# Streams of small matmuls resumed by a running account of all engines, in place of fixed sleeping times

## The chip, the cores and the metric

The kernel runs on one core of a Trainium2 chip. The time is the device time of one execution in microseconds, and the kernel before is told by the median of three runs. A core has five engines that this text names: PE (TensorE, the matmuls; PEld is its loading of weights), DVE (VectorE), ACT (ScalarE), POOL (GpSimd) and SP (SyncE, which issues most DMAs). Each works through its own instructions in order, and waits by semaphore for what others produce.

## The reference

One step of a two-layer encoder trunk. A prompt of 1024 frames with 16 meta tokens ahead of it, and 8 running streams of 16 frames, 1168 columns in all, pass through each layer. A layer normalises its input, projects it to many heads, and runs three kinds of mixers side by side: latent attention (8 heads), mLSTM (4 heads) and gated DeltaNet (4 heads); their outputs are gated and projected back. The two recurrences go chunk by chunk, each chunk needing the state of the one before:

```
def step(S, xs_c):                                       # gated DeltaNet
    A   = where(strict, b * (k @ k^T) * gamma, 0)
    u,w = triangular_solve(A + I, [b * v, b * exp(G) * k])
    delta = u - w @ S
    o = (q * exp(G)) @ S + ((q @ k^T) * gamma) @ delta
    S = exp(G_last) * S + (k * exp(G_last - G))^T @ delta
    return S, o

def step((C, n, m), xs_c):                               # mLSTM
    m_t = max(b + m, max_s dmat);  w_inter = exp(b + m - m_t)
    qk  = (q @ k^T) * exp(dmat - m_t)
    num = w_inter * (C @ q) + qk @ v;  den = w_inter * (n @ q) + sum(qk)
    h   = num / max(|den|, exp(-m_t))
    C, n = g_state * C + v g_tok k^T,  g_state * n + g_tok k
```

Everything is float32 in and out. The outputs are the activations of both kinds of streams, the new latents and rotary keys, and the states.

## The kernel before, in words

The frames are kept transposed: 128 features on the partitions, 1168 columns in three slices (400, 384, 384). The recurrences use one meta chunk of 16 columns, eight chunks of 128 (0 to 8) and one for the samples (9).

*Dense work.* Most of PE's time is the projection of the layer's input (`projs`, `part`, L610 and following): for each 128 output features and each slice 24 accumulating matmuls into a PSUM tile `pa`, with weights split into a high part (`wh`, fp32r) and bfloat16 (`wb`). The output projection (`out_first`, `out_proj`) is of the same kind. This chain, `main()`, is called the filler.

*Streams.* Everything else is a generator: `gates` (L709, gates and decays of all heads), `gdn(h)` (L895, one DeltaNet head), `mlstm(h)` (L1191), `gfin` and `mfin` (finish of a batch of chunks), `rstd`, `normx`, `normy` (the norms, L476 to L565), and attention (`prep`, `gload`, `att_m`, `att`, `samp_*`). A stream records instructions and then says `yield y`: it wants to sleep for y microseconds.

*What sets the order.* `Weave.run` (L269 to L305) writes everything out before the chip runs. It keeps a planned time of PE, `W.t`, which only `mm` and `tr` (L360 to L374) advance, each by a guess from the size. It takes the first stream in its list whose sleep is over; if there is none, three dense matmuls. So a sleep is the amount of other PE work that is put between a step and the next one. The order of recording is the priority by which a list scheduler then orders each engine, and `gate` (L378) ties some DVE, ACT, POOL and SP instructions to the place on PE after which they were recorded.

*A chunk step of `gdn`* (L1097 to L1168): k·S and q·S into `psS`; DVE forms r0 from it (L1124); two transposes of the next chunk (`pre`); sleep YA = 0.84; PE multiplies the inverse U with r0 (L1129); DVE scales the result to dl (L1131); sleep YB = 0.70; PE multiplies kd and dl (L1135), DVE forms the new state (L1140); sleep 0.7. A step of `mlstm` has one such exchange through DVE (L1278, from PSUM; sleep YM = 0.8).

*The inverse* of a DeltaNet head: DVE solves blocks of 16 rows (L950 to L966); the two results T and U go to DRAM (`td`, `ud`) and come back in another layout (L970 to L974; sleeps 9.0, 2.12 and 5.00), ACT and DVE mask them (L982, L983), and six merge steps (L990 to L1050) join blocks of 16 to 32, 64 and 128, each a group of small matmuls, one DVE or ACT operation on its result, and a sleep YI = 2.5. Other fixed sleeps are YF = 7.70 ahead of `finish` (L882, its matrix work waits for L1176 to L1320's scales), YT = 5.30, YN = 9.20 and 2.70 in the norms (ahead of the broadcast of the scales, whose operand L508 makes), 0.45 to 8.0 in `gates` (L820 is DVE's in it).

`split` (L436) makes the high and low part of a loaded weight; its second half runs on DVE or POOL (L441).

## Time and profile before

| | |
|---|---|
| median of three runs | 2652.36 us (2650.05 to 2653.49) |
| the profiled execution, whole | 2655.11 us |
| its span, first to last instruction | 2653.3 us |
| PE busy | 2494.3 us, 94% of the span |
| DVE, ACT, POOL busy | 58%, 42%, 29% |
| granted TensorE clock, mean | 0.976 |

A busy share over the whole span hides stages, so the rows further below also show two windows of 50 us, one of them in attention. The line numbers in the profile are those of the kernel before; `L361` is the matmul helper, `L372` the transpose helper, so matmuls of all streams carry these lines, and are told apart by their tiles and by who releases them. `pa` are PSUM tiles of dense work, `pb` those of streams, `wk` working tiles, `pg` pages, `sm` small columns.

### The profile page before, as it was taken

To read this page: it belongs to the slowest core of one execution; us is meant where nothing else is said; L and a number is where in the kernel's file an instruction comes from. 1 tells how busy PE (TensorE), PEld (TensorE's weight loads), DVE (VectorE), ACT (ScalarE), POOL (GpSimd) and SP (SyncE) were. 2 spreads that over 40 slices of the span, in tenths; PEclk is the share of its full clock that TensorE was granted. 3 is DMA by queue.
4 is the path that set the end of the run, shared out by engine and by line. 5 is a ranking of instruction groups with operands and counts; after the bars stand their busy time and mean duration, and the time that the engine had idled before them with its cause. 6 is when DMAs were issued, how large, how long until landed. Compare 5 with 4: busy or idle time off the path is not lost. (4 is left out here: it accounts for less than half of the span.)

```text
span 2653.3 us, 45522 instructions
## 1 busy us (share of the span) xinstructions
PE 2494.3 (94%) x17310; PEld 2154.2 (81%) x17310; DVE 1529.8 (58%) x3716; ACT 1115.5 (42%) x2635; POOL 763.2 (29%) x865
## 2 busy tenths in 40 slices
PE   6999999999999999979998999999999999999997
PEld 4887888878878888779977888788788788887896
DVE  6667465465453476655565784755743526665636
ACT  5363444444442433443343544444444434334612
POOL 3112222122123542232341222221221245322414
PEclk9999999999999999989999999999999999998998
DMA  3212112121113734464422121221211255444832
GB/s 130 67 40 76 51 52 83 51 69 49 60 59 113 201 105 122 124 215 160 153 79 57 43 74 52 61 73 51 69 52 57 84 148 162 116 115 149 281 117 80
DMA packets 158411, 258.67 MB, mean 97 GB/s; under 512 B 48704, under 2 KB 110768, under 8 KB 158192
## 3 DMA queue, kind: packets, MB, share of 16 engines
q1 hardware_dynamic: 152224, 247.59, 30.2%
q0 software_dynamic: 1856, 3.86, 0.7%
q10 hardware_dynamic: 4112, 4.30, 0.7%
q8 instruction: 137, 2.24, 0.4%
q14 instruction: 82, 0.67, 0.1%
HBM read 190.77 MB, written 64.92 MB: 96 GB/s over the span
## 5 line engine op out<-in xcount | busy, mean ns | idle before, releaser
L361 PE MATMUL pa<-pg,wh 128*128 128x384 f32 (+3 forms) x6324 | 1320.5, 352 | 25.5 <-DVE wk L1423 8.8
L361 PEld LDWEIGHTS pa<-pg,wh 128*128 128x128 f32 x6324 | 1108.2, 190 | 69.4 <-DVE wk L1423 9.4
L361 PE MATMUL pb<-pg,pg 128*128 128x352 f32 (+26 forms) x1908 | 427.4, 339 | 17.7 <-DVE sm L1552 4.4
L361 PE MATMUL pa<-pg,wb 128*128 128x384 bf16 (+1 forms) x2208 | 422.1, 331 | 6.2 <-POOL pg L544 4.2
L361 PEld LDWEIGHTS pb<-pg,pg 128*128 128x128 f32 (+7 forms) x1908 | 302.5, 189 | 71.1 <-issue 14.9
L361 PEld LDWEIGHTS <-wb 128*128 128x128 bf16 x2208 | 202.0, 98 | 142.4 <-issue 30.4
L361 PE MATMUL pb<-wk,pg 128*128 128x128 f32 (+4 forms) x2168 | 224.2, 250 | 21.2 <-ACT wk L983 5.5
L441 POOL TENSOR_TENSOR wh<-wf,wh 128x1024 fp32r<-128x1024 f32 (+1 forms) x61 | 144.1, 2363 | 325.1 <-ACT wh L437 318.7
L361 PEld LDWEIGHTS pb<-wk,pg 128*128 128x128 f32 (+3 forms) x2168 | 195.2, 162 | 43.0 <-issue 16.8
L1589 ACT ACTIVATE wk<-pb 128x320 f32<-128x320 f32 (+8 forms) x288 | 113.9, 406 | 244.9 <-PE pb L361 221.4
L361 PE MATMUL pa<-wk,pg 128*128 128x320 f32 (+8 forms) x576 | 192.5, 420 | 1.8 <-ACT wk L1589 1.3
L437 ACT CAST wh<-wf 128x1024 fp32r<-128x1024 f32 (+1 forms) x122 | 126.4, 1036 | 126.0 <-PE pa L361 110.7
L1552 DVE TENSOR_REDUCE sm<-pb 128x1 f32<-128x348 f32 (+9 forms) x232 | 107.8, 493 | 102.3 <-PE pb L361 89.6
L1612 DVE RECIPROCAL wk<-pa 64x320 f32<-64x320 f32 (+2 forms) x48 | 110.6, 2305 | 51.1 <-PE pa L361 50.4
L361 PE MATMUL pb<-wk,wk 32*32 32x16 f32 (+6 forms) x1776 | 110.7, 216 | 15.3 <-POOL wk L1285 5.6
L868 DVE SCALAR_TENSOR_TENSOR pg<-pg,vec,pg 128x1192 f32<-128x1192 f32 x72 | 107.2, 1504 | 18.3 <-ACT pg L866 18.0
L1530 POOL TENSOR_TENSOR pg<-pg,pg 64x520 fp32r<-64x520 f32 (+1 forms) x64 | 87.0, 1370 | 104.8 <-ACT pg L1529 91.1
L693 ACT COPY pg<-pa 128x384 f32<-128x384 f32 (+1 forms) x108 | 52.0, 481 | 134.4 <-PE pa L361 133.2
L457 ACT CAST wb<-wf 128x1024 bf16<-128x1024 f32 x92 | 96.2, 1045 | 26.3 <-PE pa L361 20.6
L441 DVE TENSOR_TENSOR wh<-wf,wh 128x1024 fp32r<-128x1024 f32 (+1 forms) x61 | 78.9, 1293 | 47.3 <-ACT wh L437 47.0
L361 PEld LDWEIGHTS pa<-wk,pg 128*128 128x128 f32 (+1 forms) x576 | 98.8, 195 | 5.9 <-ACT wk L1589 1.8
L361 PEld LDWEIGHTS pb<-wk,wk 32*32 32x32 f32 (+2 forms) x1776 | 73.2, 122 | 33.9 <-issue 9.4
(298 smaller groups left out, 3196.3 us busy)
## 6 DMA issues: line engine op xcount, KB each, us to landing
wf<-win SPq DMA_DIRECT2D x92, 512.0 KB
pg<-latT SPq DMA_DIRECT2D x32, 520.0 KB
pg<-latN SPq DMA_DIRECT2D x32, 512.0 KB
wf<-wout SPq DMA_DIRECT2D x24, 512.0 KB
xa<-wk SPq DMA_DIRECT2D x40, 192.0 KB
mix<-pg SPq DMA_DIRECT2D x12, 584.0 KB
pg<-mix SPq DMA_DIRECT2D x12, 584.0 KB
mix<-pg SPq DMA_DIRECT2D x12, 576.0 KB
```

Of the source, the lines that this page charges most:

```text
L361: W.last = P.matmul(out, lhsT, rhs, start=start, stop=stop)
L437: S.copy(hi, src)
L441: lo_eng.tensor_sub(lo, src, hi.bitcast(F32))
L457: S.copy(wb[:, :n], wf)
L693: S.copy(o[:, s0:s1], ps)
L868: V.scalar_tensor_tensor(y[:, :n], cb[:, j:j + n], vcol(l, "cw", 4 * ti + j), y[:, :n], op0=ALU.mult, op1=ALU.add)
L1530: G.tensor_sub(lo, raw, hi.bitcast(F32))
L1552: V.tensor_reduce(mx[:LEN[c], 3 * c + i_:3 * c + i_ + 1], ps[:LEN[c], :n1 - x_], axis=AX.X, op=ALU.min)
L1589: S.activation(pt[:m, :b - a], ps, AF.Exp, scale=-1.0)
L1612: V.reciprocal(rc, po[d, :w])
```

## The change

The planned time is replaced by an account of every engine. `Clocks` keeps the time at which each written range of a tile is expected to be done, a clock for PE, and lists of busy stretches for DVE, ACT, POOL and SP, into whose gaps a new instruction is fitted. `Engine` wraps each engine's interface, so every recorded instruction is entered with a cost by its size. `due(tiles)` gives the time at which these tiles are expected, and `due()` the time at which the last instruction that this step recorded is; a stream that yields it sleeps until `W.t` reaches that. `ring` makes a new PSUM or working tile wait for the one whose place it takes. `W.t` is now PE's clock in the account, so it also grows by PE's expected waits, and matmul costs are set anew.

Fixed sleeps that become `due`: those of the norms, `gates`, `gdn`, `mlstm`, `gfin` and `mfin`. Those of attention and of the sample streams stay in numbers. No instruction is added or removed; all of them keep their operands, save that four halves of `split` change engine, as it alternates between two.

```
+class Clocks:
+    HOP = 90.0
...
+    def run(self, eng, outs, ins, ns, late=0.0, queue=None):
+        t = max([0.0] + [self.ready(a) + self.HOP for a in ins]
+                + [self.after.get(self.where(a)[0], 0.0) for a in outs])
+        if eng == "PE":
+            t = max(t, self.clk["PE"])
+            self.clk["PE"] = t + ns
+        else:
+            t = self.fit(eng, t, ns)
+        e = t + ns
+        if queue is not None:
+            e = max(e, self.clk.get("dma", 0.0)) + queue
+            self.clk["dma"] = e
+        e += late
+        for a in outs:
+            self.write(a, e)
...
+        if eng != "PE":
+            self.last = max(self.last, e)
+        return t
...
+class Engine:
+    COST = {"DVE": (150.0, 1.08), "ACT": (224.0, 0.83), "POOL": (200.0, 2.1)}
...
+            if name == "dma_start":
+                n = aps[0].size() if callable(aps[0].size) else aps[0].size
+                c.run(kind, outs, ins, 60.0 if kind != "POOL" else 600.0, 1900.0, n * 4 / 260.0)
+            else:
+                n = max(x.free_size() for x in aps)
+                b, m = self.COST[kind]
+                ns = b + m * n
...
+                c.run(kind, outs, ins, ns, 60.0)
...
 class Weave:
...
                     r = next(th[0])
-                    if isinstance(r, (int, float)):
+                    if isinstance(r, At):
+                        th[1] = max(r, self.t)
+                    elif isinstance(r, (int, float)):
                         th[1] = self.t + r * 1000.0
...
+    def due(*aps):
+        return At(max([CK.ready(a) for a in aps]) + CK.HOP) if aps else At(max(CK.last, W.t) + CK.HOP)
...
         elif rhs.dtype != F32:
-            W.t += max(n / 2.4, 107.0)
+            ns = max(n * 0.4375 + 7.0, 107.0)
...
+    def pe(out, a, b, ns):
+        CK.clk["PE"] = W.t
+        CK.run("PE", [out], [a, b], ns, 160.0)
+        W.t = CK.clk["PE"]
...
-        yield 2.70
+        yield due(dg)
...
-            yield 9.0
+            yield due()
             ld(td.rearrange("c (b i) j -> (c b) (i j)", b=8), Ti)
             ld(ud.rearrange("c (b i) j -> (c b) (i j)", b=8), Ui)
-            yield 2.12
+            yield due()
             Tc, Uc = AD, ip[:, 928:1088].rearrange("p (c j) -> p c j", j=16)
             ld(Tc, td.rearrange("c s j -> s c j"))
             ld(Uc, ud.rearrange("c s j -> s c j"))
-            yield 5.00
+            yield due()
...
-            yield YI
+            yield due()
...
-                    yield YA
+                    yield due(r0)
...
-                    yield YB
+                    yield due(dl)
...
-                    yield 0.7
+                    yield due(Sst) if c < 9 else 0.7
...
-            yield YF
+            yield due(Ob)
...
-                    yield YM
+                    yield due(*([V1, VG] + ([CN] if c else [])))
```

What this does to the order is shown at three places. In these rows `L361`, `L372` and `L383` of the kernel before are `L491`, `L503` and `L340` of the changed one, and tile numbers differ between the two.

PE, layer 0, a chunk step of DeltaNet head 2. `pb809` of the kernel before is k·S and q·S (two matmuls), `pb810` the transposes, `pb819` U·r0; `pa` are dense matmuls. Before:

```order
L361 MATMUL pb809_5181<-wk807_5168,pg591_3737 128x128
L361 MATMUL pb809_5181<-wk807_5168,pg714_4360 128x128
L372 MATMUL pb810_5185<-cst_92,pg669_4083 128x128
L372 MATMUL pb810_5185<-cst_92,pg591_3737 128x128
L361 MATMUL pa798_5127<-pg15_122,wh751_4844 128x384
L361 MATMUL pa798_5127<-pg16_123,wh751_4844 128x384 x2
L361 MATMUL pa818_5219<-pg9_116,wh777_4999 128x400 x2
L361 MATMUL pa818_5219<-pg10_117,wh777_4999 128x400
L361 MATMUL pb819_5223<-wk802_5146,pg732_4563 128x128
```

In the changed kernel the same step is `pb808`, `pb809` and `pb812`:

```order
L491 MATMUL pb808_5120<-wk806_5107,pg600_3781 128x128
L491 MATMUL pb808_5120<-wk806_5107,pg714_4359 128x128
L503 MATMUL pb809_5124<-cst_92,pg684_4126 128x128
L503 MATMUL pb809_5124<-cst_92,pg600_3781 128x128
L491 MATMUL pa803_5098<-pg9_116,wh764_4900 128x400
L491 MATMUL pa803_5098<-pg10_117,wh764_4900 128x400 x2
L491 MATMUL pb812_5134<-wk793_5064,pg739_4608 128x128
```

Between the transposes and U·r0 stood six dense matmuls; now there are three.

PE, layer 1, the first merge of DeltaNet head 1. The 32 matmuls of `32x32` are the first product, the two groups of `32x16` use its masked result. Before:

```order
L361 MATMUL pb_16279<-wk_16237,pg_15886 32x32 x32
L361 MATMUL pa_16266<-pg_13452,wh_16122 128x384 x2
L361 MATMUL pa_16266<-pg_13453,wh_16122 128x384 x2
L361 MATMUL pa_16266<-pg_13454,wh_16122 128x384 x2
L361 MATMUL pa_16266<-pg_13455,wh_16122 128x384 x2
L361 MATMUL pa_16266<-pg_13456,wh_16122 128x384 x2
L361 MATMUL pa_16266<-pg_13457,wh_16122 128x384 x2
L361 MATMUL pa_16327<-pg_13450,wh_16122 128x384 x2
L361 MATMUL pa_16327<-pg_13451,wh_16122 128x384 x2
L361 MATMUL pa_16327<-pg_13452,wh_16122 128x384 x2
L361 MATMUL pb_16334<-wk_16312,wk_16237 32x16 x32
L361 MATMUL pb_16368<-wk_16237,wk_16312 32x16 x32
```

The same in the changed kernel, where the `32x32 x16` behind them begins the next merge:

```order
L491 MATMUL pa_16605<-pg_13450,wh_16392 128x384 x2
L491 MATMUL pb_16193<-wk_16171,pg_15805 32x32 x32
L491 MATMUL pa_16605<-pg_13451,wh_16392 128x384 x2
L491 MATMUL pa_16605<-pg_13452,wh_16392 128x384 x2
L491 MATMUL pb_16240<-wk_16226,wk_16171 32x16 x32
L491 MATMUL pb_16274<-wk_16171,wk_16226 32x16 x32
L491 MATMUL pb_16322<-wk_16171,pg_15805 32x32 x16
L491 MATMUL pa_16605<-pg_13453,wh_16392 128x384 x2
L491 MATMUL pa_16605<-pg_13454,wh_16392 128x384 x2
L491 MATMUL pb_16350<-wk_16226,wk_16171 32x32
L491 MATMUL pb_16350<-wk_16171,wk_16226 32x32
```

Between first product and second stood 18 dense matmuls, and now four; the next merge follows the second product with none between.

SP, layer 1, DeltaNet head 0: the way of T and U through DRAM. `td1_0` and `ud1_0` are the DRAM buffers, `MR1` another row of the gates, `wf` a weight's landing tile. Before:

```order
L383 DMA pg2578_14664<-MR1 128x9x128
L383 DMA td1_0<-pg2560_14431 80x256
L383 DMA ud1_0<-pg2560_14431 80x256
L383 DMA pg2578_14664<-MR1 128x16
L453 DMA wf2594_14881<-win 128x1024
L383 DMA pg2560_14431<-td1_0 128x10x16
L383 DMA pg2560_14431<-ud1_0 128x10x16
```

In the changed kernel:

```order
L340 DMA pg2578_14660<-MR1 128x9x128
L340 DMA pg2578_14660<-MR1 128x16
L340 DMA wf2596_14908<-win 128x1024
L340 DMA td1_0<-pg2556_14385 80x256
L340 DMA ud1_0<-pg2556_14385 80x256
L340 DMA pg2556_14385<-td1_0 128x10x16
L340 DMA pg2556_14385<-ud1_0 128x10x16
```

The stores of T and U stand behind the second load of `MR1` and the weight load, and their loads follow at once.

## Rows read from the trace of the kernel before

**Rows 1.** Head of the profile page: span, busy time and share by engine.

```profile
span 2653.3 us, 45522 instructions
...
PE 2494.3 (94%) x17310; PEld 2154.2 (81%) x17310; DVE 1529.8 (58%) x3716; ACT 1115.5 (42%) x2635; POOL 763.2 (29%) x865
```

**Rows 2.** Waits of PE by releaser: total us, times, longest us.

```profile
PE pb L361 <- DVE wk L508: 19.5, 17, 4.6
...
PE pb L361 <- POOL wk L1285: 5.6, 4, 2.3
PE pb L361 <- ACT wk L983: 5.5, 1, 5.5
...
PE pb L361 <- DVE wk L1131: 4.5, 6, 2.2
...
PE pb L361 <- POOL wk L1956: 3.8, 2, 2.8
...
PE pb L372 <- DVE pg L820: 3.4, 1, 3.4
PE pb L361 <- DVE wk L1278: 3.3, 3, 1.7
...
PE pb L361 <- DVE sm L923: 2.7, 1, 2.7
PE pb L372 <- DVE wk L1320: 2.5, 3, 1.2
...
PE pb L361 <- DVE wk L1140: 2.0, 4, 0.9
PE pb L361 <- DVE wk L1124: 2.0, 3, 1.4
```

**Rows 3.** PE's timeline, first and last stage: start, us, instruction, [idle before].

```profile
16.75 1.22 PE L361 MATMUL pb<-wk,onesr 128*128 128x400 f32 x2 [4.62 <-DVE wk L508]
...
2641.51 1.01 PE L361 MATMUL pb<-cst,wk 128*128 128x1 f32 x4 [2.82 <-POOL wk L1956]
2644.90 0.82 PE L361 MATMUL pb<-wk,onesr 128*128 128x256 f32 x2 [2.38 <-DVE wk L508]
```

**Rows 4.** Timeline of all engines, second loads of the inverse, layer 1.

```profile
1444.15 0.43 SPq L383 DMA_DIRECT2D pg<-td  x1
...
1449.93 1.08 PE L361 MATMUL pb<-wk,pg 32*32 32x32 f32 x64 [5.51 <-ACT wk L983]
```

**Rows 5.** Timeline of all engines, one chunk step of the gated DeltaNet, head 2.

```profile
466.71 0.61 PE L361 MATMUL pb<-wk,pg 128*128 128x128 f32 x4
...
467.29 1.31 PE L361 MATMUL pa<-pg,wh 128*128 128x384 f32 x6
467.36 0.35 DVE L1124 SCALAR_TENSOR_TENSOR wk<-pb,sm,wk 128x128 f32<-128x128 f32 x1 [0.84 <-PE pb L361]
...
468.44 0.38 PE L361 MATMUL pb<-wk,pg 128*128 128x128 f32 x2
```

**Rows 6.** Timeline of all engines, one merge of the inverse, layer 0.

```profile
586.17 0.42 DVE L997 TENSOR_TENSOR wk<-pb,cst 128x256 f32<-128x256 f32 x1
...
588.97 1.21 PE L361 MATMUL pb<-wk,wk 32*32 32x16 f32 x120
```

**Rows 7.** Timeline of all engines, end of a batch of chunks.

```profile
223.02 2.36 POOL L441 TENSOR_TENSOR wh<-wf,wh 128x1024 fp32r<-128x1024 f32 x1
223.09 2.31 DVE L1176 TENSOR_TENSOR sm<-sm 128x4 f32<-128x4 f32 x1 [0.88 <-POOL sm L1175]
```

**Rows 8.** Groups by line and shape: count, busy us, mean ns, idle before.

```profile
L1176 DVE TENSOR_TENSOR sm<-sm 128x1 f32<-128x1 f32 x12 | 1.9, 161 | 7.5 <-POOL sm L1175 7.5
...
L441 POOL TENSOR_TENSOR wh<-wf,wh 128x1024 fp32r<-128x1024 f32 x57 | 136.8, 2400 | 318.5 <-ACT wh L437 312.1 <-DVE wk L1890 6.3
```

**Rows 9.** Busy time by window (us, share): a recurrence and an attention stretch.

```profile
300.00:350.00 50.00, 49.66 (x351) 42.44 (x351) 24.80 (x79) 23.63 (x67) 7.69 (x10) 1.00 0.14 45
1150.00:1200.00 50.00, 43.09 (x294) 41.41 (x294) 24.20 (x44) 22.24 (x56) 16.74 (x27) 0.85 0.60 198
```

More of the change, by code (lines that the diff above doesn't have):

```diff
@@ L248, in unpack, with __init__, where, ready @@
     )
+class At(float):
+    pass
+class Clocks:
+    HOP = 90.0
+    def __init__(self):
+        self.clk = {}
+        self.busy = {}
+        self.done = {}
+        self.seen = {}
+        self.after = {}
+        self.last = 0.0
+    @staticmethod
+    def where(a):
+        t = a.tensor
+        if a.space.name == "DRAM":
+            return t.name, a.offset, a.offset + 1 + sum((n - 1) * abs(s) for s, n in a.ap)
+        lo = a.offset % a.ap[0][0]
+        hi = lo + 1 + sum((n - 1) * abs(s) for s, n in a.ap[1:])
+        return t.name, lo, hi
+    def ready(self, a):
+        name, lo, hi = self.where(a)
+        return max([e for x, y, e in self.done.get(name, ()) if x < hi and lo < y], default=0.0)
+    def write(self, a, e):
+        name, lo, hi = self.where(a)
+        self.done[name] = [w for w in self.done.get(name, ()) if not (lo <= w[0] and w[1] <= hi)] + [(lo, hi, e)]
+    def run(self, eng, outs, ins, ns, late=0.0, queue=None):
[13 more added lines that the diff above has]
+            self.write(a, e)
+        for a in ins + outs:
+            n = self.where(a)[0]
+            self.seen[n] = max(self.seen.get(n, 0.0), e)
+        if eng != "PE":
+            self.last = max(self.last, e)
+        return t
+    def fit(self, eng, t, ns):
+        q = self.busy.setdefault(eng, [])
+        while len(q) > 200:
+            q.pop(0)
+        k = len(q)
+        while k and q[k - 1][0] >= t:
+            k -= 1
+        if k and q[k - 1][1] > t:
+            t = q[k - 1][1]
+        while k < len(q) and q[k][0] < t + ns:
+            t = max(t, q[k][1])
+            k += 1
+        q.insert(k, (t, t + ns))
+        return t
+    def follows(self, new, old):
+        if old is not None:
+            self.after[new] = self.seen.get(old, 0.0) + self.HOP
@@ L308, in _build @@
 def _build(nc, tc, ctx, I, O, layers):
-    V, S, G, P = nc.vector, nc.scalar, nc.gpsimd, nc.tensor
+    W = Weave()
+    CK = W.clocks
+    V, S, G = (Engine(e_, n_, CK) for e_, n_ in ((nc.vector, "DVE"), (nc.scalar, "ACT"), (nc.gpsimd, "POOL")))
+    P, SY = nc.tensor, Engine(nc.sync, "SP", CK)
+    def due(*aps):
+        return At(max([CK.ready(a) for a in aps]) + CK.HOP) if aps else At(max(CK.last, W.t) + CK.HOP)
     cp = ctx.enter_context(tc.tile_pool(name="const", bufs=1))
@@ L823, in gates @@
             D1["MR"] = 1
-            yield 1.23
+            yield due()
             ps = pb()
@@ L909, in gdn @@
             V.memset(hs, 1.0)
-            yield 8.0
+            yield due(kT)
             yield from need(1)
@@ L1061, in gdn @@
             QD = D
-            yield 4.0
+            yield due(qT)
             for b in BATCHES:
```

119 lines of the change are left out of this document (73 added, 46 removed).

## Prediction

> **What bounds the kernel now.** I read the head of the page first, then PE's waits by releaser, then timelines around the waits and around one step of each kind, then the groups by shape and two windows. PE is busy 2494.3 of 2653.3 us [rows 1]: at most 159.0 us can be won, and only where PE waits. A step that a stream finishes sooner gives nothing by itself, because the same matmuls are still to be done; a step that is put too close behind its operand costs the whole difference, because PE takes its instructions in order. So the change is priced by two lists: waits of PE that an earlier or later place takes away, and steps whose cover of dense matmuls becomes too thin.
>
> The waits that belong to streams with a new sleep are the eleven rows of [rows 2]: 19.5 + 5.6 + 5.5 + 4.5 + 3.8 + 3.4 + 3.3 + 2.7 + 2.5 + 2.0 + 2.0 = 54.8 us. Three of their instances lie where no dense work is left to put between, at the beginning and at the end: 4.62 + 2.82 + 2.38 = 9.8 us [rows 3]. That leaves 45.0 us in reach. The other waits, such as those for attention, keep their fixed sleeps. A recurrence stretch has PE at 49.66 of 50 us and an attention stretch at 43.09 [rows 9], so where most of the new sleeps are there is least to win.
>
> **Waits that go.** Every time below is that of the profiled execution, 2655.11 us; it lies 2.75 above the median of 2652.36, and I take that off at the end.
>
> Three waits stand alone, and the changed order removes the cause of each. The longest is 5.51 us, where the masking on ACT waits for T to come back from DRAM, a load issued at 1444.15 and used at 1449.93 [rows 4]. Two fixed sleeps, 2.12 and 5.00, stand for that way; the account prices each DMA and puts 31 to 50 us of PE work between the solve and the first merge, where 28 to 31 stood (both counted from the order at the durations of the trace). That the stores now stand behind one weight load on SP delays them by one issue of that queue, about 0.4 us as the issue in [rows 4], and the added cover is larger. The second is 3.4 (L820, a step of `gates`), the third 2.7 (L923, ahead of `finish`) [rows 2]. Together 5.5 + 3.4 + 2.7 = 11.6 us, taken in full.
>
> The rest, 45.0 − 11.6 = 33.4 us, is 12.5 us of L508 (19.5 less 4.62 and 2.38), the L1285, L1320 and L1956 rows, and the chunk steps. The account knows the operand of each (`due(dg)`, `due(r0)`, `due(vB)`), so its expectation should fit where a fixed number was too short; but it knows nothing of what the list scheduler moves afterwards, and it charges by size alone. I take half, 16.7 us. Bounds: none and all, that is 0 and 33.4.
>
> Sum of what goes: 28.3 us, between 11.6 and 45.0 if the three are sure, from 0 if they are not.
>
> **Waits that come.** First the chunk steps. Around U·r0 the row of before reads: products ready at about 467.32 (466.71 + 0.61), DVE's L1124 from 467.36 for 0.35, so r0 at 467.71; PE takes it at 468.44 [rows 5]. Slack 0.73 us, with six dense matmuls of 1.31 us between [rows 5]. The order of the changed kernel has three there, so half of that 1.31, 0.65 us, is gone: slack 0.08. So a typical step still just fits, and nothing is lost by it; but any other DVE operation ahead of L1124 now shows. Over both layers, four heads and the chunks these steps are 72 of L1131, 72 of L1124 and 64 each of L1140 and L1278, 272 in all, of which the rows of before count 6 + 3 + 4 + 3 = 16 waits with 4.5 + 2.0 + 2.0 + 3.3 = 11.8 us, 0.74 each [rows 2]. The median cover in the order falls from six to three at L1124 and L1140, stays six at L1131 and falls from nine to four in `mlstm`. I take as many again as there were: 16 × 0.74 = 11.8 us. Bounds: 0, if the expectation is good to 0.08 us on average; and, if DVE is found at work by every second of the 200 steps with thinner cover (its busy share is 58% [rows 1]) and each then costs 0.74, 100 × 0.74 = 74 us.
>
> Second the merges. Before, DVE's mask takes 0.42 us from 586.17 and the next product starts at 588.97 [rows 6]: 588.97 − 586.59 = 2.38 us of slack. In the order, covers of 17 or 18 dense matmuls become 2 to 10. At the 0.22 us of one dense matmul (1.31 over six [rows 5]) ten are 2.2 and two 0.4 us, against a need of about half a microsecond. Of 8 heads × 6 = 48 steps I take every sixth to wait half a microsecond: +4. Bounds 0 and 48 × 0.5 = 24.
>
> `finish` has a cover of 5 to 8 us after against nearly 10 before; its operand chain on DVE and POOL needs less than that in most rows, and I add nothing beyond the rest above. Sum of what comes: 11.8 + 4 = 15.8, bounds 0 and 98.
>
> **Kept as it is, but shifted.** Attention and samples keep their numbers, yet sleep against a `W.t` that also counts PE's waits, so a given number now covers less PE work. An attention window has 50 − 43.09 = 6.9 us without PE [rows 9]; one and a half such windows more or less make ±10. I take 0, since neither sign is shown. The granted clock there is 0.85 and in a recurrence stretch 1.00 [rows 9]; the order of work in attention is hardly touched, so I price no change of it. Four halves of `split` change engine; 2.40 us each on POOL [rows 8], and neither engine is the bound: nothing.
>
> **Sum.** 2655.1 − 28.3 + 15.8 = 2642.6; less 2.75 this is 2640 us by the runs' median.
>
> **What the account cannot see.** POOL's half of a weight split began at 223.02 for 2.36 us, and a DVE operation on four columns that began at 223.09 took 2.31 [rows 7], where the same line on one column takes 0.161 on average over 12 [rows 8]. It ended with the other: a stall of 2.15 us that depends on when the two meet. The account charges DVE by columns and never meets POOL. The Trainium skill ("SBUF — State Buffer", section "Who interferes with whom") says that a DVE instruction with two SBUF inputs and a GpSimd one that reads SBUF exclude each other, and that the one issued second blocks fully. That row agrees. By the rule the thinner covers are wrong whenever a split runs; by the sum above they are wrong only at random.
>
> **Rivals.**
>
> *Slower, by stalls of DVE behind POOL's splits under thin covers.* There are 57 such splits of 2.40 us [rows 8]. Before, a slack of 0.7 to 2.4 us [rows 5, 6] hid part of a stall; after, 0.08 hides none. POOL is busy 29% of the span [rows 1]; if one split in three catches DVE ahead of a step, that is 19 × 2.15 = 41 us more: 2655.1 − 28.3 + 15.8 + 41 − 2.75 = 2681. It decides from 12.5 / 2.15, about six such catches, on. For it: the row of 223.09, and the halved covers. Against it: the L1124 and L1140 steps read one operand from PSUM, so they are stopped only when an operation ahead of them on DVE is.
>
> *No change, given back.* Only the three single waits go (11.6) and the chunk steps bring 11.8: −11.6 + 11.8 = 0, 2652. For it: half of what I let go in the rest rests on the account being right, and the list scheduler still moves about a fifth of the matmuls away from where they were recorded, after as before.
>
> *All of the reach.* The account is right everywhere and no new wait comes: 2652.4 − 45.0 = 2607. For it: the sleeps before were one number for all instances of a step. Against: 16 of 272 chunk steps waiting is already a low share.
>
> **How the numbers follow.** Forecast 2640 (its own range 2630 to 2650, by the ±10 of attention): 0.38. All of the reach, 2607: 0.12. No change: 0.20. Slower: 0.30. A difference under 0.2% (5.3 us) is what a measurement of this kernel cannot tell from no change. Faster by more: 0.38 + 0.12 = 0.50; within: 0.20; slower: 0.30. The range reaches from the full reach to the slower rival, 2607 to 2681, and leaves out the upper bounds of the new waits (98 us) and a gain in stages that I did not price, together about 0.2.
>
> **What would show it.** The first product of the inverse in layer 1, head 0, no longer waits for L983's counterpart, and the L820 and L923 waits are gone (the 11.6). L508's row falls from 19.5 towards 7 us plus half of 12.5, some 13. The chunk rows (L1131, L1124, L1140, L1278) stay near 16 to 25 waits and below 20 us; over 50 us in them and longer DVE operations beside POOL's splits would make the slower rival true. The merge steps show waits of half a microsecond where none were. PE's busy time stays within some us of 2494. I am wrong if the attention windows change by more than 10 us, or if the gain comes from where PE did not wait for a stream with a new sleep.

## The result and the profile after

The changed kernel is slower: 2695.1 us in the median of four runs (2691.2 to 2701.8), against 2651.2 for the kernel before in the same comparison; the ratio is 1.0168, with a 95% interval of 1.0143 to 1.0194. The forecast was 2640 and its range ended at 2681.

The head of the page, as in [rows 1]:

```profile
span 2690.3 us, 45584 instructions
...
PE 2517.2 (94%) x17310; PEld 2168.1 (81%) x17310; DVE 1534.6 (57%) x3716; ACT 1115.8 (41%) x2635; POOL 774.4 (29%) x865
```

PE's time without work is span less busy: 2690.3 − 2517.2 = 173.1 us, 14.1 more than the 159.0 of before. But busy time grew as well, by 2517.2 − 2494.3 = 22.9 us, for the same 17310 matmuls. The mean granted clock fell from 0.976 to 0.967. The share of the span that the lower clock takes is 0.024 × 2653.3 = 64 us before and 0.033 × 2690.3 = 89 after, which is 25 more. So of the 37.0 us by which the span grew, about 14 are waits and about 23 are work at a lower clock. The other executions agree on the clock: in all four of the changed kernel its mean is 0.963 to 0.967, in the fifty of the kernel before that were timed beside the kernels below it is 0.975 to 0.981.

Most of what the clock lost beyond the kernel before, it lost in one stage, from the 4400th to the 7600th matmul into a `pa` tile: the end of layer 0's output projection and layer 1's recurrences. The whole stage in one window, the kernel before first (us from the start, length, then busy of PE, PEld, DVE, ACT, POOL with counts, then granted clock, DMA share and GB/s):

```profile
1258.20:2048.10 789.90, 752.99 (x5861) 645.89 (x5860) 467.42 (x1320) 345.26 (x820) 200.73 (x215) 0.99 0.23 69
1269.10:2077.10 808.00, 770.68 (x5860) 656.60 (x5859) 460.53 (x1319) 344.37 (x819) 209.28 (x216) 0.97 0.22 68
```

PE idled 36.9 us in it before and 37.3 after, but the same matmuls took 17.7 us longer, out of 22.9 in the whole kernel. So the sum of the waits does not tell this loss. What changed there is their length: waits of 1.5 us and more were 6 with 16.0 us and became 10 with 24.2.

The waits of PE by releaser answer to [rows 2]. In the changed kernel every instruction outside PE carries the line of the wrapper, L340, so the releasers' lines no longer tell the steps apart; L491 is the matmul and L503 the transpose:

```profile
PE pb L491 <- DVE wk L340: 43.1, 33, 10.4
PE pb L503 <- DVE wk L340: 18.2, 12, 4.0
PE pb L491 <- DVE pg L340: 17.3, 14, 2.6
...
PE pb L491 <- ACT wk L340: 8.3, 5, 3.5
...
PE pb L491 <- POOL wk L340: 2.0, 3, 0.9
```

The second row is `finish`, where PE transposes the scaled block, a `wk` tile, into `pb`. Before, its largest row was L1320's 2.5 us [rows 2]; now it is 18.2 us in 12 waits, the longest 4.0. For the other steps I matched the trace's PE records one to one with the recorded program, in which each matmul's step is known. By that sum the chunk steps did what the expectation was to do: waits of `mlstm` fell from 15.5 to 3.6 us and those ahead of U·r0 from 4.8 to 0.6, and in `gates` from 7.3 to 1.4. Ahead of `finish` they rose from 4.0 to 18.3, at the first product of a DeltaNet head from 0 to 6.4, in the output projection from 13.7 to 19.6, and ahead of the norms' broadcast from 20.1 to 24.2. Short waits became fewer and long ones more: of the waits over 0.05 us, those under 1.5 us were 136 and became 103, and 69.9 us became 58.0; of 1.5 us and more 28 became 41, and 81.0 us became 105.5.

What one such long wait is made of shows the timeline around the 4.0 us wait ahead of `finish` in layer 0:

```profile
548.40 0.16 DVE L340 TENSOR_TENSOR sm<-sm 128x4 f32<-128x4 f32 x1
548.52 1.46 DVE L340 SCALAR_TENSOR_TENSOR pg<-pg,vec,pg 128x1192 f32<-128x1192 f32 x1
...
549.89 0.17 DVE L340 TENSOR_SCALAR sm<-sm 128x4 f32<-128x4 f32 x1
550.14 1.01 POOL L340 TENSOR_TENSOR sm<-sm,neg 128x4 f32<-128x4 f32 x1 [5.22 <-DVE sm L340]
...
554.09 0.35 DVE L340 SCALAR_TENSOR_TENSOR pg<-pg,sm,cst 128x128 f32<-128x128 f32 x1 [4.03 <-DMA pg<-GR]
554.35 0.16 DVE L340 TENSOR_TENSOR sm<-sm 128x4 f32<-128x4 f32 x1
554.43 1.45 DVE L340 SCALAR_TENSOR_TENSOR pg<-pg,vec,pg 128x1192 f32<-128x1192 f32 x1
555.80 0.16 DVE L340 TENSOR_SCALAR sm<-sm 128x4 f32<-128x4 f32 x1
...
556.02 0.67 DVE L340 TENSOR_TENSOR wk<-wk,sm 128x512 f32<-128x512 f32 x1
...
556.74 1.11 PE L503 MATMUL pb<-cst,wk 128*128 128x128 f32 x4 [3.98 <-DVE wk L340]
...
557.65 4.69 PE L491 MATMUL pa<-pg,wb 128*128 128x384 bf16 x14
```

The scale of a finished batch is a chain of short operations on `sm` columns, with one power on POOL (550.14), and then the scaling of the block (556.02). POOL was done at 551.15. DVE took the next step of the chain only at 554.35, because it stood at an operation of another head (554.09) for 4.03 us, until that head's gate row had come by DMA. Then a 1.45 us operation on a page, no part of the chain either, went between two of its steps. DVE takes its instructions in their order, so a step that is ready cannot go ahead of one that waits. The account fits a new instruction into any gap of DVE's planned list, also a gap in front of one that waits for a DMA.

Behind that wait stands the last row of the timeline, 14 matmuls in 4.69 us. Two windows, of 10 and 3 us, show the clock around it:

```profile
545.00:555.00 10.00, 7.76 (x56) 6.60 (x54) 4.47 (x12) 3.84 (x12) 1.01 (x1) 1.00 0.35 119
558.00:561.00 3.00, 3.00 (x11) 1.48 (x10) 3.00 (x7) 1.06 (x2) 2.28 (x5) 0.50 0.00 0
```

Three microseconds in which PE had no gap at all were run at 0.50, the 1.2 GHz level. The wait cost 3.98 us, and then half of the time at the lower level on top. As a difference between the two kernels this place counts for little, though. In the kernel before, PE waited near the same place for POOL's L1285, 2.31 and 1.26 us, and the clock fell behind these waits too:

```profile
558.71 0.92 PE L361 MATMUL pb<-wk,wk 128*128 128x387 f32 x2 [2.31 <-POOL wk L1285]
562.00:564.00 2.00, 2.00 (x6) 1.26 (x5) 1.64 (x8) 0.00 (x0) 0.00 (x0) 0.50 0.40 41
```

The merges show the other kind of place, layer 1 at 1612:

```profile
1611.10 0.97 PE L491 MATMUL pa<-pg,wh 128*128 128x384 f32 x4
...
1613.55 0.21 PE L491 MATMUL pb<-wk,wk 32*32 32x32 f32 x1 [1.30 <-issue]
1613.69 1.33 PE L491 MATMUL pa<-pg,wh 128*128 128x384 f32 x3
1614.95 1.06 PE L491 MATMUL pb<-wk,wk 32*32 32x32 f32 x44
1615.94 1.65 PE L491 MATMUL pa<-pg,wh 128*128 128x384 f32 x4
1617.52 1.97 PE L491 MATMUL pb<-wk,pg 64*64 64x64 f32 x16
1619.41 1.65 PE L491 MATMUL pa<-pg,wh 128*128 128x384 f32 x4
```

The merge groups now have four dense matmuls between them. Four such took 0.97 us at 1611.10 and 1.65 at 1615.94, beside 64x64 products, after 1.30 us of idle time to which the profile gives no releaser (`issue`). Three windows of layer 1's recurrences after, and the same stretches of time before, which hold partly other work:

```profile
1450.00:1500.00 50.00, 43.79 (x530) 35.15 (x528) 22.80 (x36) 21.14 (x39) 9.45 (x10) 0.91 0.16 39
1500.00:1550.00 50.00, 45.66 (x290) 38.31 (x289) 34.01 (x116) 26.59 (x96) 6.81 (x14) 0.89 0.16 46
1600.00:1650.00 50.00, 43.32 (x514) 34.25 (x512) 20.20 (x58) 21.01 (x53) 11.00 (x10) 0.86 0.09 22
```

```profile
1450.00:1500.00 50.00, 49.50 (x593) 42.55 (x594) 29.58 (x69) 26.24 (x67) 9.20 (x8) 0.95 0.06 22
1500.00:1550.00 50.00, 47.36 (x345) 39.70 (x344) 39.80 (x149) 25.96 (x82) 16.49 (x22) 1.00 0.21 69
1600.00:1650.00 50.00, 47.84 (x335) 41.46 (x335) 21.92 (x60) 20.12 (x53) 9.17 (x7) 1.00 0.20 56
```

In the second and third, where the kernel before ran at 1.00, the clock is 0.89 and 0.86.

The wait for T and U from DRAM, which the prediction let go in full [rows 4], became another one:

```profile
1451.05 0.42 SPq L340 DMA_DIRECT2D td<-pg  x1
...
1454.75 0.38 SPq L340 DMA_DIRECT2D pg<-td  x1
...
1458.97 0.75 PE L491 MATMUL pb<-wk,pg 32*32 32x32 f32 x64 [3.50 <-ACT wk L340]
```

5.51 us became 3.50. In SP's queue the loads stand right behind the stores, but they were issued 3.70 us after the first of them. Before, T's load (1444.15, [rows 4]) followed its store by 1.78 us:

```profile
1442.37 0.32 SPq L383 DMA_DIRECT2D td<-pg  x1
```

### The profile page after: what moved, and what is told of

It reads as the page before. It is cut to its first block, busy times and chain, and to the rows that moved or that the text cites. A ratio compares the mean times of both kernels' runs of the same rounds, so it can differ in the third digit from the quotient of the medians.

```text
span 2690.3 us, 45584 instructions
## 1 busy us (share of the span) xinstructions
PE 2517.2 (94%) x17310; PEld 2168.1 (81%) x17310; DVE 1534.6 (57%) x3716; ACT 1115.8 (41%) x2635; POOL 774.4 (29%) x865
## 5 line engine op out<-in xcount | busy, mean ns | idle before, releaser
L491 PE MATMUL pa<-pg,wh 128*128 128x384 f32 (+3 forms) x6324 | 1334.0, 355 | 33.7 <-DVE wk L340 12.0
L491 PEld LDWEIGHTS pa<-pg,wh 128*128 128x128 f32 x6324 | 1115.9, 191 | 81.6 <-issue 14.3
L491 PE MATMUL pb<-pg,pg 128*128 128x128 f32 (+24 forms) x1908 | 409.4, 336 | 22.9 <-DVE pg L340 8.8
L491 PE MATMUL pa<-pg,wb 128*128 128x384 bf16 (+1 forms) x2208 | 422.9, 332 | 6.0 <-ACT pg L340 2.7
L491 PEld LDWEIGHTS pb<-pg,pg 128*128 128x128 f32 (+7 forms) x1908 | 302.2, 192 | 76.3 <-issue 18.7
L491 PEld LDWEIGHTS <-wb 128*128 128x128 bf16 x2208 | 204.1, 99 | 145.4 <-issue 32.3
L340 POOL TENSOR_TENSOR pg<-pg,pg 128x384 fp32r<-128x384 f32 (+6 forms) x172 | 229.8, 1348 | 297.1 <-ACT pg L340 272.7
L340 POOL TENSOR_TENSOR wh<-wf,wh 128x1024 fp32r<-128x1024 f32 (+1 forms) x63 | 150.6, 2390 | 378.3 <-ACT wh L340 369.3
L340 ACT ACTIVATE wk<-pb 128x320 f32<-128x320 f32 (+10 forms) x312 | 122.3, 399 | 281.1 <-PE pb L491 238.5
L491 PE MATMUL pb<-wk,pg 128*128 128x128 f32 (+4 forms) x2168 | 226.7, 251 | 10.2 <-ACT wk L340 4.5
L491 PEld LDWEIGHTS pb<-wk,pg 128*128 128x128 f32 (+3 forms) x2168 | 193.7, 162 | 35.8 <-issue 17.0
L340 ACT COPY pg<-pa 128x384 f32<-128x384 f32 (+5 forms) x252 | 106.6, 433 | 229.9 <-PE pa L491 222.0
L491 PE MATMUL pa<-wk,pg 128*128 128x320 f32 (+8 forms) x576 | 195.1, 424 | 0.0
L340 ACT CAST wh<-wf 128x1024 fp32r<-128x1024 f32 (+1 forms) x122 | 126.4, 1036 | 158.7 <-PE pa L491 143.2
L340 ACT CAST pg<-pg 128x384 fp32r<-128x384 f32 (+6 forms) x316 | 166.2, 578 | 53.3 <-DVE pg L340 17.4
L340 POOL TENSOR_TENSOR sm<-sm,neg 128x4 f32<-128x4 f32 (+2 forms) x72 | 78.7, 1093 | 377.4 <-DVE sm L340 365.7
L340 DVE TENSOR_TENSOR pg<-pg,pg 128x384 fp32r<-128x384 f32 (+8 forms) x154 | 141.2, 951 | 41.2 <-ACT pg L340 25.7
L340 DVE RECIPROCAL wk<-pa 64x320 f32<-64x320 f32 (+2 forms) x48 | 110.7, 2305 | 64.4 <-PE pa L491 63.9
L340 POOL TENSOR_TENSOR wk<-wk,wk 64x320 f32<-64x320 f32 (+6 forms) x90 | 88.4, 983 | 169.0 <-DVE wk L340 130.4
L340 DVE TENSOR_REDUCE sm<-pb 128x1 f32<-128x348 f32 (+9 forms) x232 | 105.6, 491 | 54.4 <-PE pb L491 46.6
L340 DVE SCALAR_TENSOR_TENSOR pg<-pg,vec,pg 128x1192 f32<-128x1192 f32 (+2 forms) x102 | 130.9, 1297 | 7.5 <-ACT pg L340 7.0
L340 DVE TENSOR_TENSOR wh<-wf,wh 128x1024 fp32r<-128x1024 f32 (+1 forms) x59 | 78.1, 1324 | 96.8 <-ACT wh L340 96.5
```

The source lines that it names most:

```text
L340: r = f(*a, **k)
L491: W.last = P.matmul(out, lhsT, rhs, start=start, stop=stop)
```

## The experiments

Four theories were put to the test one after another. F: the expectations ahead of `finish` and of a head's first product are too early. M: the merges with thin covers lower the clock. W, later split as P: the new planned time itself (matmul costs, and expected waits that count as time passed) breaks the sleeps. T: the old table of numbers fits one order, and any other order of the same work loses. A fifth pair, C and L, is about what a wait costs.

| kernel | median us | ratio to before (95%) | PE idle | PE busy | clock |
|---|---|---|---|---|---|
| changed | 2695.1 | 1.0168 (1.0143 to 1.0194) | 173.1 | 2517.2 | 0.967 |
| `finish` in numbers | 2707.6 | 1.0209 (1.0181 to 1.0237) | 179.8 | 2530.1 | 0.962 |
| inverse in numbers | 2727.2 | 1.0280 (1.0263 to 1.0297) | 193.0 | 2536.5 | 0.958 |
| all in numbers, new planned time | 2693.2 | 1.0156 (1.0133 to 1.0179) | 183.4 | 2507.5 | 0.971 |
| chunks by account, rest in numbers | 2752.7 | 1.0372 (1.0356 to 1.0388) | 214.2 | 2537.6 | 0.961 |
| all by account, no planned waits | 2679.9 | 1.0103 (1.0083 to 1.0123) | 165.5 | 2513.3 | 0.969 |
| before with new matmul costs | 2667.1 | 1.0065 (1.0043 to 1.0088) | 166.9 | 2493.4 | 0.976 |
| changed, with margins | 2697.2 | 1.0161 (1.0137 to 1.0185) | 168.5 | 2531.1 | 0.962 |
| before, sleeps 8% longer | 2664.3 | 1.0048 (1.0033 to 1.0064) | 155.1 | 2514.0 | 0.970 |
| before, long waits added | 2746.6 | 1.0360 (1.0340 to 1.0381) | 216.8 | 2525.8 | 0.963 |
| before, shorter waits added | 2789.5 | 1.0520 (1.0501 to 1.0539) | 246.8 | 2539.2 | 0.960 |
| old planned time, chunks by account | 2718.7 | 1.0245 (1.0217 to 1.0273) | 192.3 | 2525.0 | 0.963 |
| old planned time, all by account | 2679.7 | 1.0117 (1.0089 to 1.0144) | 169.5 | 2504.5 | 0.971 |
| the same with margins | 2723.6 | 1.0269 (1.0246 to 1.0291) | 180.7 | 2538.1 | 0.956 |
| before, sleeps jittered, 1 | 2668.5 | 1.0069 (1.0046 to 1.0091) | 165.7 | 2513.5 | 0.970 |
| before, sleeps jittered, 2 | 2645.3 | 0.9964 (0.9953 to 0.9976) | 151.1 | 2495.3 | 0.976 |
| before, sleeps jittered, 3 | 2676.1 | 1.0086 (1.0064 to 1.0108) | 159.7 | 2512.4 | 0.969 |
| only mLSTM's `finish` by account | 2671.1 | 1.0076 (1.0051 to 1.0100) | 166.4 | 2504.9 | 0.974 |
| gates, norms, inverse by account | 2681.2 | 1.0126 (1.0102 to 1.0150) | 168.8 | 2510.8 | 0.969 |

Idle, busy and clock are those of each kernel's profiled execution; ratios are of the runs that were timed together. A profiled execution can lie off the median: it took 2662.1 us with the new matmul costs (the fastest of ten, which reach to 2687.3), 2671.2 with 8% longer sleeps (the slowest of five) and 2681.0 with jitter 1 (the slowest of six).

**Undoing parts of the change.** `finish` put back to numbers:

```
-            yield due(Ob)
+            yield YF
...
-            yield due(Hh)
+            yield YF + 1.0
```

> The changed kernel with the two sleeps ahead of `finish` put back to 7.70 and 8.70; all else as changed. Theory F (the expectation of the scaled block ahead of `finish` is too early: PE's waits there grew from 4.0 to 18.3 us, and the granted clock falls behind some of them): the 14 us of waits go and some 5 us of clock with them, 2695 becomes about 2676. Theory M (the inverse of each DeltaNet head, now with thin covers, lowers the granted clock in layer 1): at most the 4 to 5 us, 2690. Theory W (the new planned time itself, with PE's waits in it and new matmul costs, is what costs): 2692.

It got slower, 2707.6, outside all three forecasts. Of the row of `finish`, 18.2, there was left

```profile
PE pb L503 <- DVE wk L340: 12.4, 8, 6.3
```

so in this order the old number, slept against the new planned time, does not cover the step. F is not enough. But W's reading, that the number has changed its meaning, is not shown by this row: with all sleeps in numbers and the same planned time (two kernels below) the waits ahead of `finish` are 3.4 us by the matching of steps. What else stands on DVE in that order counts too.

The start of a head, the inverse and its merges put back to their 15 numbers (8.0, 4.0, 3.30, 2.5, 2.5, 9.0, 2.12, 5.00, YT, YI):

> The changed kernel with the sleeps at the start of a DeltaNet head, in the inverse and in its merges put back to numbers (8.0, 4.0, 3.30, 2.5, 2.5, 9.0, 2.12, 5.00, 5.30, 2.5 six times); all else as changed. Theory M: of the 18.7 us that the stage of layer 1's recurrences grew by, the 15.4 us of clock and the 6.4 us of waits at the first product of a head go: about 2675. Theory F: 2688 to 2692, only the waits at the first product go. Theory W: 2690.

Slower still by 32 us than the changed kernel, and outside all three forecasts. The stage of layer 1's recurrences, from the same matmul to the same matmul as above, has no better clock with the merges' covers in numbers again:

```profile
1300.60:2113.20 812.60, 767.51 (x5861) 656.46 (x5860) 455.42 (x1319) 345.60 (x819) 208.90 (x216) 0.97 0.22 68
```

That speaks against M, but it is no clean test of it, since the numbers brought waits of their own. The waits ahead of the first merge, where T and U come back, were 18.9 us in this kernel by the matching of steps (4.6 in the changed one): 9.0 + 2.12 + 5.00 of the new planned time is too little for the way through DRAM.

All sleeps back to numbers, with the new planned time kept:

> All sleeps put back to the numbers of before, but slept against the new account's planned time (its matmul costs, and PE's expected waits in it). Theories F and M: the loss is in the new sleeps, so 2650 to 2658, like before. Theory W: the planned time alone makes most of the loss, 2675 to 2695.

2693, like the changed kernel, and in W's range: with none of the expectations in use, the planned time alone makes as large a loss. By the matching of steps the waits for T and U are 17.4 us here, and 4.0 in the kernel before with the new matmul costs alone (below), so at this place the numbers do cover less once planned waits count as time passed. The chunk steps alone by the account:

> Numbers everywhere save in the chunk steps of both recurrences, which sleep by the account. Theories F and M: waits in the chunk steps fell from about 25 to about 10 us in the changed kernel, and this keeps that gain without the losses: 2635 to 2642. Theory W: 2665 to 2690, the planned time costs as in the run with all numbers and the chunk steps give back 10 to 15.

Wrong by 60 us and more for every theory. It is the slowest of the orders; the chunk steps' own waits did not fall in it, and the waits for T and U were 21.7 us, both by the matching of steps.

**The planned time taken apart.** Expected waits no longer advance PE's planned time, all else as changed:

```
         CK.run("PE", [out], [a, b], ns, 160.0)
-        W.t = CK.clk["PE"]
+        W.t = W.t + ns
```

> The changed kernel, but PE's planned time advances by the matmul's own cost alone, as before the change, and not by the waits that the account expects (it plans 268 us of them; the changed kernel's trace has 164 us without PE). Theory P (planned waits that do not happen count as cover, so streams come back with too little dense work in between): 2655 to 2675. Theory T (the old numbers fit one order; any other order of the same work loses): 2680 to 2710. Theory F (only the expectations ahead of `finish` and at the first product of a head are too early): unchanged, 2685 to 2700.

2679.9, a gain of 15 on the changed kernel. That is 5 us above P's range and at the lower edge of T's, so it does not decide between them. Only the new matmul costs, in the kernel before:

```
...
-            W.t += max(n / 2.4, 107.0)
+            W.t += max(n * 0.4375 + 7.0, 107.0)
...
```

> The kernel before with the new matmul costs in its planned time (fp32r about 9% dearer, bfloat16 and fp32 2%), nothing else: no account, the old sleeps, which now cover some 6% less dense work. Theory P: the costs alone lose little, 2650 to 2660. Theory T: 2665 to 2695, as any shift of the order. Theory F says nothing of it beyond about 2655.

2667.1, at the lower edge of T. With the run of all numbers these make a table of four, all with the new costs: numbers without planned waits 2667, numbers with them 2693, expectations without them 2680, expectations with them 2695. By these differences planned waits cost 26 and 15 us, the expectations 13 and 2, the costs of matmuls 15. All but the 26 are within what an order that differs by chance can cost (−8 to +22 us, see the jittered kernels), so they are sizes, and not yet causes.

**Margins and plain shifts.** 2.0 us more ahead of `finish` and of the first product:

```
...
-            yield due(Ob)
+            yield At(due(Ob) + 2000.0)
...
```

> The changed kernel with 2.0 us added to the expectation in three places: ahead of `finish` (both recurrences) and ahead of the first product of a DeltaNet head. Theory F: their waits, 18.3 and 6.4 us, fall to about 5 and 0 and the clock lost behind them by 5 or more: 2665 to 2675. Theory P: 2685 to 2695, the same waits turn up at other steps. Theory T: 2680 to 2710 without a direction.

The row of `finish` fell from 18.2 to

```profile
PE pb L503 <- DVE wk L340: 6.8, 6, 2.2
```

and PE's idle time by 4.6 us in all, yet the kernel is not faster: its busy time grew by 13.9. F is refuted as the cause of the time; the time lies in T's range. Every sleep of the kernel before 8% longer (`r * 1080.0` in place of `r * 1000.0`):

> The kernel before with every sleep given in numbers made 8% longer, nothing else: more cover everywhere. Theory T: 2665 to 2690, worse although no cover became thinner. Theories P and F: thicker covers cost PE nothing, 2645 to 2658.

```profile
span 2669.1 us, 45503 instructions
...
PE 2514.0 (94%) x17310; PEld 2164.5 (81%) x17310; DVE 1508.1 (56%) x3716; ACT 1118.4 (42%) x2635; POOL 766.7 (29%) x865
```

By the medians it is 12 us slower: 2664.3, just under T's range and 6 above that of P and F. In the profiled execution, the slowest of its five, PE waits 3.9 us less than before, as thicker covers should have it, and its busy time is 19.7 longer. So the loss is one of the clock, without more waiting; why the clock fell is not shown.

**What a wait costs.** In the kernel before, DVE copies an operand onto itself in the middle of a dense accumulation, and the next accumulation is kept behind it (the same 207 copies in both kernels):

```
...
+                    if i_ == 13 and R["np"] % 12 == 6:
+                        for _ in range(9):
+                            V.tensor_copy(x_[k][:, s0:s0 + 256], x_[k][:, s0:s0 + 256].bitcast(F32))
...
```

> The kernel before, plus deliberate waits: in every twelfth dense accumulation nine DVE copies of a moving operand onto itself (256 columns) stand between the thirteenth and the fourteenth matmul, and the next accumulation is kept behind. About 15 to 20 waits of some 2.5 us, less what stream matmuls fill. Theory C (a long wait costs its length and then lower granted clock, some 1.7 us or more each): the sum of PE's waits grows by 30 to 45 and the clock's loss by 25 to 40: 2705 to 2735. Theory L (a wait costs its length alone): 2680 to 2700, clock's loss within 8 us of before's 60.

and three copies in every fourth accumulation:

> The same number of DVE copies in three times as many places: three copies in every fourth dense accumulation, about 45 to 60 waits of some 0.9 us. Theory C: the sum of waits grows by as much as with the long ones or more, 30 to 50, and the clock's loss by under 15: 2685 to 2715, less than the long ones. Theory L: the same as the long ones or more, 2680 to 2705.

PE's waits for these copies were, with the nine copies (total us, times, longest):

```profile
PE pa L361 <- DVE pg L620: 34.7, 16, 5.1
```

and with the three:

```profile
PE pa L361 <- DVE pg L620: 70.6, 38, 8.2
```

The shorter ones were not short: 70.6 us in 38 is 1.9 each, against 34.7 in 16, 2.2 each. So the two do not tell long from short, and both times, 2746.6 and 2789.5, lie above the ranges of C and of L. They do tell that a wait costs more than its length: idle time grew by 57.8 and by 87.8 us, more than by the waits for the copies alone, and busy time by 31.5 and 44.9 on top, at a clock of 0.963 and 0.960. A microsecond of added waiting cost another 0.5 of work at the lower clock here; L allowed 8 us in the first of the two.

**The old planned time kept.** Old matmul costs, no planned waits, chunk steps alone by the account:

> The account is kept, but PE's planned time advances by the old matmul costs and without expected waits, as before the change, and only the chunk steps of both recurrences sleep by the account; all other sleeps are the old numbers, so they cover what they covered before. Theory P (the planned time is what broke the numbers): the chunk waits of 25 us fall by half, the rest is as before, 2635 to 2652, which would beat both kernels. Theory T (the old table fits its own order only): 2660 to 2680, as with all sleeps 8% longer.

2718.7: the numbers mean what they meant before and it is still 67 us slower, outside both theories. By the matching of steps the waits for T and U grew from 5.5 to 21.7 us, half of the 33.3 by which PE's idle time grew, although their sleeps are the old ones. Everything by the account:

> The old matmul costs and no expected waits in PE's planned time, but all sleeps that the change turned into expectations stay so. Theory P: better than the run with the new costs and no planned waits (2680), 2650 to 2670, since the old costs run 6 to 9% slow against the chip and so every expectation gets that much more cover. Theory T: 2670 to 2690, like that run.

2679.7, as with the new costs, and in T's range. One wait stands out, again for T from DRAM in layer 1:

```profile
1584.12 1.08 PE L491 MATMUL pb<-wk,pg 32*32 32x32 f32 x64 [15.21 <-ACT wk L340]
```

With margins at the places whose waits had grown (2.0 ahead of `finish` and the first products, 6.0 after the substitution, 3.0 after the loads):

> Old matmul costs, no expected waits in PE's planned time, all new sleeps by the account, and a margin at the places whose waits grew: 2.0 us ahead of `finish` and of the first products of a DeltaNet head, 6.0 after the substitution, 3.0 after the loads of T and U. Theory P/F: the one wait of 15.2 us at the inverse of layer 1 and most of the 10.9 us ahead of `finish` go, 2680 becomes 2645 to 2662. Theory T: 2670 to 2695, other places take their turn.

That wait is gone, and it is slower by 44, outside both ranges: busy time grew by 33.6 at a clock of 0.956, and ahead of `finish` the waits went from 10.9 to 15.4 us by the matching of steps. Margins are no remedy.

**Other orders without an account.** Each sleep of the kernel before times its own factor between 0.85 and 1.15:

```
-                        th[1] = self.t + r * 1000.0
+                        self.seed = (self.seed * 1103515245 + 12345) % 2147483648; th[1] = self.t + r * (850.0 + 300.0 * self.seed / 2147483648.0)
```

> The kernel before, with every sleep given in numbers multiplied by its own pseudo-random factor between 0.85 and 1.15; no account, old costs, the mean sleep unchanged. Theory T (the old table of numbers fits its one order; other orders of the same work wait longer at a few places): 2660 to 2690. Theory P/F (the account's own errors make the loss): 2645 to 2658, since no sleep is off by more than 15%.

> As the first jittered kernel, with other pseudo-random factors. Theory T: 2660 to 2690. Theory P/F: 2645 to 2658.

> As the first jittered kernel, with other pseudo-random factors. Theory T: 2660 to 2690. Theory P/F: 2645 to 2658.

Two fall into T's range; the second, at the lower end of the other range, is faster than the kernel before, 0.9964 (0.9953 to 0.9976), and so beats both kernels, by chance. Its page:

```profile
span 2646.4 us, 45529 instructions
...
PE 2495.3 (94%) x17310; PEld 2157.8 (82%) x17310; DVE 1518.4 (57%) x3716; ACT 1118.6 (42%) x2635; POOL 768.1 (29%) x865
```

Idle time is 7.9 us less than before, at the same clock. With the 8% and the new costs there are now five orders that differ from the old one only in sleeping times: 1.0065, 1.0048, 1.0069, 0.9964 and 1.0086, on average 1.0046 or 12 us.

**One expectation at a time**, on the old planned time and with the other numbers untouched. Only the mLSTM heads' `finish`:

> The kernel before in order and planned time (old costs, no expected waits, all old numbers), save that the `finish` of the mLSTM heads alone sleeps by the account instead of 8.70. Theory F (this expectation comes too early because the scale's short operations on DVE and POOL stand between others' longer ones): the waits ahead of `finish` grow from 4.0 to 8 to 14 us and the clock loses a few more: 2660 to 2678. Theory T (it is one more order like the jittered ones, whose waits there stayed at 1.6 to 4.1): 2645 to 2676 without growth at `finish`.

```profile
PE pb L491 <- DVE wk L340: 51.5, 40, 10.4
...
PE pb L503 <- DVE pg L340: 3.4, 1, 3.4
```

The second row is the one of `gates` (L820 before). The row that would be `finish` (L503, released by DVE through `wk`) is gone from the waits altogether; 4.0 us became 0. F is wrong for this expectation taken alone, and T's forecast fits: 20 us slower without waits at `finish`. Idle time grew by 7.4 at other steps of both recurrences, busy time by 10.6.

Gates, norms and the inverse's way through DRAM:

> The same base, with the gates, the norms and the inverse's way through DRAM by the account, all else the old numbers: the places at which the prediction let waits go. The prediction's own step: the waits at L826 (3.4), at the first product of the inverse (5.5) and part of the norms' 20.1 go, 2630 to 2645. Theory T: these go, but the order loses as much elsewhere, 2650 to 2675.

```profile
PE pb L491 <- DVE wk L340: 47.1, 33, 10.1
...
PE pb L503 <- DVE wk L340: 11.4, 10, 2.4
```

By the matching of steps the waits of the prediction's first term went as forecast: L826 3.4 to 0, first merge 5.5 to 0, ahead of the norms' broadcast 20.1 to 10.8, together 18.2 us. The row of `finish`, whose number is untouched here, shows what came instead (11.4), the DeltaNet chunk steps grew by 12.7 by the matching, and the whole is 30 us slower, 6 above T's range. This is the clearest run on where a gain goes.

## Why the prediction was wrong

**The bound.** PE was the bound, and the reach of 45 us was rightly read. But pricing PE's waits at their length alone was wrong: added waits brought work at a lower clock, 31.5 us of it behind 57.8 and 44.9 behind 87.8, and no term of the sum held that. Two steps failed. One is "so I price no change of it" in the part on what is kept: granted clock, valued at 0 and measured at about +23 us of the +37. That sentence speaks of attention. The recurrences, read at 1.00, got no price for the clock at all, and in layer 1's stage of them came 17.7 us of the 22.9. The other is the balance of waits: the sum had them fall by 28.3 − 15.8 = 12.5 us, and they rose by 14.1. The largest part of that is `finish`, put at nothing.

**Waits that go.** The three single waits were 11.6 us in full. L820's went. L923's wait stood ahead of U·r0, and not, as the prediction has it, ahead of `finish`: its row names L361, a matmul, where `finish` transposes; that place fell from 4.8 to 0.6 in all. The wait for T went from 5.51 to 3.50. The longer cover that the order gave it did not hold on the chip; the way from the first store to T's load alone took 3.70 us instead of 1.78, where the prediction had added 0.4. Of the rest, taken at half: the norms did not fall (20.1 to 24.2) in the changed kernel, though they did when planned waits were left out (9.4), and the recurrences' chunk steps fell by more than half. The term was right in kind: in the last experiment its waits at L826, the first merge and the norms came to 18.2 us less.

**Waits that come.** The chunk steps were to bring 11.8 us; their waits went down. The covers of three matmuls did suffice, as the slack of 0.08 us had said. The merges brought a few waits, near the +4. What was missed is "`finish` [...] I add nothing": it brought 14 us, the largest new term; the first products of a head (+6.4) stood in no term either. I compared the cover of `finish`, 5 to 8 us, with the need of a typical row, and did not look at what else stands between the short operations of its scale on DVE: an operation that waited 4.03 us for a DMA held up the ready step behind it, and a gap that the account sees in front of such an operation was not open on the engine. That is shown for one of the waits, the longest.

**Kept as it is, but shifted.** Taken at 0 within ±10; the stages of attention and output projections of the two layers grew by about 5 us and by 4 to 8 (from the 3200th to the 4400th dense matmul, and from the 7600th to the end; it depends on which matmuls are counted as dense), together 9 to 12, the edge of its bounds or just beyond. With the old planned time the first grew by 5 to 6 as well and the second by −2 to 3 (all by the account). That the planned time now counts waits was named there, and it was a right place to look: by the experiments planned waits cost 15 to 26 us. That sleeping streams are let out by waits that the chip does not have fits the waits for T and U (17.4 us against 4.0), and is not shown elsewhere.

**The rivals.** The slower one came near in time (2681 for 2695) by a mechanism that its own rows refute: the chunk steps did not wait more, and DVE's busy time, which a stall behind a split lengthens as in [rows 7], grew by 1534.6 − 1529.8 = 4.8 us in all, where it needed 41. The nearness in time is luck. The 0.30 that the prediction gave to a slower kernel rested on that mechanism alone. The rule of the Trainium skill that it leaned on ("SBUF — State Buffer", "Who interferes with whom") is not contradicted by this; it was not what decided the time.

**What is shown, and what is open.** Shown: the loss is in two parts, waits and clock; added waits cost more than their length; the new planned time makes as large a loss without the expectations; most of the predicted waits do go. Shown also: five orders with shifted sleeps and no account lose 12 us on average, between −8 and +22. So some part of the loss of any account-made order may be only that the old table had been the better of many. The kernels that wait by the account, or sleep against its planned time, lose 20 to 100; all but the one with a single expectation (20) lose more than any of the five. Not shown is that waits are the whole cause of the lower clock: with all sleeps 8% longer, and in layer 1's recurrences of the changed kernel, the clock fell although PE did not wait longer in sum. Open is as well why the kernels with only the chunk steps by the account lose 67 and 100, and which single step's error makes the rest: each undone part moved the waits elsewhere. The four halves of `split` that changed engine were not tried alone.

## What to carry to other kernels

Where an engine is 94% busy and a table of times sets its order, price a wait with the slower clock behind it, and look at the single waits: their sum does not tell the loss. A planned clock and the sleeps that are set against it are one thing: change its unit and all numbers that stay have changed too. Before a scheduler is judged by one order, time a few orders that differ by chance, since here that alone was worth −8 to +22 us.

## What the runs showed that I had not expected

In ten of the profiles (the kernel before and the first nine of the table) I counted waits of PE of 1 us and more and asked whether a stretch at the 1.2 GHz level lay in the wait or in the 2 us behind it: so it was for 22% of 198 waits of 1.0 to 1.5 us, 40% of 145 of 1.5 to 2 us, and 76% of 226 longer ones. That is what stands beside waits, and no proof that each made its stretch. And twice a kernel with less idle time was no faster: with all sleeps 8% longer PE idled 155.1 us where before's idled 159.0, and took 12 us more by the medians; with margins it idled 168.5 where the changed kernel idled 173.1, and took 2 us more, which is within the spread of both.
